# Scores of an attention mixer from 32- and 64-row features in place of stacked 128-row copies

## The chip, the cores and the metric

The kernel runs on one core of a Trainium2 chip. The time is the device time of one execution in microseconds, the lower the better. The engines are PE (matmul), with its weight loads shown apart as PEld, DVE (elementwise work and reductions), ACT (activation functions and copies), POOL (elementwise work) and SP, which issues most of the DMAs.

## The reference

A diffusion backbone of two layers on 256 context tokens and 512 latent tokens, 768 tokens in all, 1024 wide. In each layer one projection feeds three groups of heads that run side by side:

```python
def diff_mixer(...):                 # 4 heads, 2 components of 32 dims each, v of 64
    def attend(q, k, v):
        s = jnp.einsum('bqhcd,bkhcd->bhcqk', q, k) * scale
        p = jax.nn.softmax(s, axis=-1)
        p = p[:, :, 0] - lam * p[:, :, 1]
        return jnp.einsum('bhqk,bkhe->bqhe', p, v)
...
def gqa_attend(q, k, v):             # 6 query heads on 2 key/value heads, 64 dims
    s = jnp.einsum('bqhgd,bkhd->bhgqk', qg, k) * dh ** -0.5
    p = jax.nn.softmax(s, axis=-1)
    o = jnp.einsum('bhgqk,bkhd->bqhgd', p, v)
...
def step(state, xs):                 # gated delta rule: 6 heads of 64 dims, both directions
    v_new = u_i - jnp.einsum('bhck,bhkv->bhcv', w_i, state)
    o_i = jnp.einsum('bhck,bhkv->bhcv', qd_i, state) + jnp.einsum('bhij,bhjv->bhiv', qk_i, v_new)
    state = state * gl_i[..., None, None] + jnp.einsum('bhck,bhcv->bhkv', kd_i, v_new)
```

Latent queries read all 768 keys, context queries the 256 context keys. The last layer needs no context queries. The outputs of the three groups go through one output projection, and a SwiGLU block ends the layer.

## The kernel before

**Numbers in two parts.** Every matmul that must be exact works on split numbers: `hi` is the value rounded to the type fp32r, and `lo` is the value less `hi`. A product is hi·hi + hi·lo + lo·hi. `split` makes the two parts: ACT copies (and so rounds), DVE subtracts.

**The attention stage of a layer.** Its heads are worked in five pairs, in the order `HORD` = 2, 0, 3, 1, 4. Pairs 0 and 1 are two differential heads each; pairs 2, 3 and 4 are two grouped-query heads each, one on either key/value head. The names below are those of the trace's tiles.

- Preparing a differential pair (`attn_prep`): q and k of the pair are loaded (`dq`, `dk`), and `to_feat` transposes them with PE (tile `exp`) and splits them into `qT` and `kT`, hi and lo, with features on the rows: 32 rows for each of 4 components. `stack4` then makes for each component a copy on all 128 rows: PE multiplies the 32 rows by the constant matrix `pick` (tile `stk`; one matmul for the hi, one for the lo part, for 256 and for 512 tokens), and DVE (256 tokens) or ACT (512) copies the result to `qs` or `ks`. The rows of `qs` are [qh, qh, ql, ql], those of `ks` [kh, kl, kh, kl].
- Preparing a grouped-query pair: `stack2` transposes, and copies the 64 rows of each head to both halves of `gqs` (hi in one half, lo in the other) and of two tiles `gks` (hi twice, lo twice), in small operations on 64 rows. The keys are made once in a layer.
- A block (`attend`) is one pair with one tile of 128 queries: a layer-0 pair has six, four with 768 keys and two with 256; a layer-1 pair has four with 768. For each component `scores` fills one of two score buffers (`S`, each of two halves of 384 keys), taken in turn: one matmul for each half on the stacked rows of a differential component, two of a grouped-query head. `softmax` takes the negated maximum on DVE (`nm`) and the exponential with its sum on ACT (`P`). For a differential head DVE then combines the two components (`cR`, and `P<-P,cR`, "the combining step" below). PE transposes `P` three tiles at a time (`pt`), DVE and ACT copy it (`PT`), PE multiplies with the values (`pv`), ACT copies (`OTs`), PE transposes back, and DVE scales into `O`.

**What sets the order.** `mixers` walks through `PLAN`, which mixes the attention's items (`a0` to `a10`) with those of the delta rule: `s0` to `s11` are its twelve steps (tile `scan`, which ends the chain from step to step, and `ops`, its outputs), `p` and `v` prepare it (`mg`, `wps`, `ups`), `o` writes its outputs. `ASTEP` says where in a pair's blocks (`a`) the next pair is prepared: `f` runs the first part of `attn_prep` and `t` the second. A scheduler then orders each engine's instructions by dependences and priorities; the `scan` steps go out at a raised priority. The pools' buffer counts (`ATTN`, here `t` for the stacked copies, `f` for features, `p` for `P`, `q` for `PT`, `g` for `gks`) bound how far ahead the work can run. Each engine executes its queue in order, so that an instruction that waits holds all behind it.

Of the kernel before, what the change touches and what calls it, by code (L numbers as in the profile page):

```python
# [10 lines left out]
F32 = mybir.dt.float32  # L11
# [55 lines left out]
PROJS = (6, 5)  # L67
ATTN = (dict(t=10, f=4, p=4, q=3, v=2, d=2, w=2, g=4, u=1),
        dict(t=10, f=3, p=4, q=4, v=2, d=2, w=2, g=4, u=1))

# [24 lines left out]
class Net:  # L95
# [995 lines left out]

    def to_feat(self, src, t0, name):

        hi, lo = (self.slot(name, F32R, tag="f") for _ in range(2))
# [8 lines left out]
    def pick_setup(self):  # L1103

        self.pick = self.R.tiny("pick", [128, 4, 128], F32R)
        raw = self.slot("pickraw", tag="d")[:, :512]
        self.dma(raw, self.A["pick"])
        self.cp(self.pick.rearrange("p a b -> p (a b)"), raw)

    def parts_of(self, t0):  # L1110

        return ((t0, 2), (2, NT)) if t0 < 2 else ((2, NT),)

    def stack4(self, feat, c, kind, t0, name):

        x = self.slot(name, F32R, tag="t")
        r = slice(32 * c, 32 * c + 32)
        for a, b in self.parts_of(t0):
            ps = self.ring("stk")[:, :128 * (b - a)]
            w = slice(128 * a, 128 * b)  # L1120
            for hl in range(2):
                self.mm(ps, self.pick[r, 2 * kind + hl], feat[hl][r, w], hl == 0, hl == 1)
            if a < 2:
                self.v.tensor_copy(x[:, w], ps)
            else:
                self.cp(x[:, w], ps)
        return x

    def stack2(self, src, t0, name, k):


        out = [[self.slot(name, F32R, tag="g" if k else "t") for _ in range(2 if k else 1)] for _ in range(2)]
        for a, b in self.parts_of(t0):
            ps = self.ring("exp")
            w = slice(128 * a, 128 * b)
            for i in range(a, b):
                self.tr(ps[:, 128 * (i - a):128 * (i - a) + 128], src[:, i])
            for c in range(2):
                own, other = slice(64 * c, 64 * c + 64), slice(64 - 64 * c, 128 - 64 * c)
                p = ps[own, :128 * (b - a)]  # L1140
                hi, lo = out[c][0], out[c][-1]
                self.cp(hi[own, w], p)
                if k:
                    self.cp(hi[other, w], p)
                    self.sub(lo[own, w], p, hi[own, w].bitcast(F32))
                self.sub(lo[other, w], p, hi[own, w].bitcast(F32))
        return out

# [25 lines left out]
    def attend(self, l, pair, O, qts):  # L1174

        for qt in qts:
            nk = TOK if qt >= 2 else CTX
            nkb = nk // 128
            PTs = []
            Z = self.tiny("Z", [128, 2, 2], bufs=4)  # L1180
            for hd, (comps, V) in enumerate(pair):
                Ps = [self.softmax(self.scores(pr, qt, nk), nk, Z[:, hd, ci:ci + 1]) for ci, pr in enumerate(comps)]
                P = Ps[0]
                if len(comps) == 2:
                    c = self.tiny("cR", [128, 1], bufs=4)
                    self.v.reciprocal(out=c, in_=Z[:, hd, 1:2])
                    self.stt(c, c, self.lam[:, l:l + 1], Z[:, hd, 0:1], ALU.mult, ALU.mult)
                    self.stt(P[:, :nk], Ps[1][:, :nk], c, P[:, :nk], ALU.mult, ALU.add)
                PT = self.slot("PT", tag="q")
                for i, k0 in enumerate(range(0, nk, 384)):  # L1190
                    n = min(384, nk - k0)
                    ps = self.ring("pt")
                    for k in range(0, n, 128):
                        self.tr(ps[:, k:k + 128], P[:, k0 + k:k0 + k + 128])
                    if i < EVD[l][len(comps) - 1]:
# [7 lines left out]
            for kb in range(nkb):  # L1203
                for c in range(2):
                    self.mm(pv[64 * c:64 * c + 64, :128], pair[c][1][:, kb], PTs[c][:, 128 * kb:128 * kb + 128], kb == 0, kb == nkb - 1)
            OT = self.R.tiny("OTs", [128, 128], bufs=2)
# [5 lines left out]
    def attn_prep(self, l, i):  # L1212


        t0 = 2 if l == DEPTH - 1 else 0
        if i < 2:
            q = self.load_tok(self.dqk[:, :, 128 * i:128 * i + 128], t0, "dq")
            k = self.load_tok(self.dqk[:, :, 256 + 128 * i:256 + 128 * i + 128], 0, "dk")
            q = self.to_feat(q, t0, "qT")
# [5 lines left out]
            yield [(comps[2 * c:2 * c + 2], vs[:, :, 64 * c:64 * c + 64]) for c in range(2)]  # L1225
            return
        if self.gks is None:
            self.gks = self.stack2(self.load_tok(self.dkv[:, :, 0:128], 0, "gk"), 0, "gks", True)
# [345 lines left out]
def shape_consts():  # L1574
# [26 lines left out]

    pick = np.zeros((4, 32, 4, 4, 32), f)
    for j, at in enumerate(((0, 1), (2, 3), (0, 2), (1, 3))):
        for b in at:
            pick[:, :, j, b] = np.eye(32, dtype=f)
    return {"ident": np.eye(128, dtype=f), "pick": pick.reshape(128, 512), "masks": masks.reshape(128, 768), "mloc": mloc,
            "negm": np.concatenate([negm.reshape(128, 128), masks[:, 2:4].reshape(128, 256)], 1), "blk2": blk2,
# [58 lines left out]
```

## Time and profile before

| | us |
| --- | --- |
| median of the three runs | 2182.35 |
| lowest, highest | 2180.88, 2187.04 |
| the profiled execution | 2187.43 |
| its span, first to last instruction | 2185.6 |

The profile is of one execution. The page's first part gives each engine's busy time and its share of the span. A view by stretches gives, for a stretch of the span, the busy time of each engine with its number of instructions in brackets, then the granted TensorE clock as a share of full speed (1.00 is the upper of its two levels, 2.4 GHz, and 0.50 the lower, 1.2 GHz), the busy share of the DMA engines and what they moved; it can be restricted to the instructions of one tile. The timeline has, for each run of like instructions of one engine, the start in us, the time it took, the engine, the line, the operation, the output and input tiles, the size, the count (xN), and in square brackets the idle time before it and what ended that. The matmuls of one timeline row may not stand next to each other in time where another row's lie between. Over the whole execution the mean granted clock is 0.943.

In this execution layer 0's attention stage lies between about 330 and 620 us, and layer 1's between about 1500 and 1745 us.

### The profile page before, as it was taken

To read this page: it belongs to the slowest core of one execution; us is meant where nothing else is said; L and a number is where in the kernel's file an instruction comes from. 1 tells how busy PE (TensorE), PEld (TensorE's weight loads), DVE (VectorE), ACT (ScalarE), POOL (GpSimd) and SP (SyncE) were. 2 spreads that over 40 slices of the span, in tenths; PEclk is the share of its full clock that TensorE was granted. 3 is DMA by queue.
4 is the path that set the end of the run, shared out by engine and by line. 5 is a ranking of instruction groups with operands and counts; after the bars stand their busy time and mean duration, and the time that the engine had idled before them with its cause. 6 is when DMAs were issued, how large, how long until landed. Compare 5 with 4: busy or idle time off the path is not lost. (4 is left out here: it accounts for less than half of the span.)

```text
span 2185.6 us, 36979 instructions
## 1 busy us (share of the span) xinstructions
PE 2020.9 (92%) x14786; PEld 1672.6 (77%) x14786; DVE 1325.2 (61%) x2223; ACT 823.8 (38%) x1609; POOL 525.0 (24%) x768
## 2 busy tenths in 40 slices
PE   7999877998889999999999989977899799999998
PEld 3788766776668888888888888865676598888887
DVE  6755774575845747565757457687767664443444
ACT  5433315464744321212122344423475653222223
POOL 2403579331014100000000350367323030000002
PEclk9999987698999999999999989987798999999999
DMA  8354434221062324343424411444212242222321
GB/s 296 121 176 132 156 109 113 47 73 35 26 227 78 116 87 154 110 131 102 155 91 140 134 56 48 133 127 125 51 47 60 86 165 77 100 85 92 106 98 61
DMA packets 167596, 236.46 MB, mean 108 GB/s; under 512 B 75328, under 2 KB 109248, under 8 KB 167424
## 3 DMA queue, kind: packets, MB, share of 16 engines
q10 hardware_dynamic: 46160, 144.92, 20.2%
q1 hardware_dynamic: 121264, 89.18, 13.4%
q8 instruction: 116, 1.90, 0.3%
q14 instruction: 56, 0.46, 0.1%
HBM read 198.00 MB, written 36.04 MB: 107 GB/s over the span
## 5 line engine op out<-in xcount | busy, mean ns | idle before, releaser
L185 ACT ACTIVATE whi<-raw 128x1024 fp32r<-128x1024 f32 (+4 forms) x246 | 220.7, 912 | 499.6 <-PE dps L188 207.3
L161 DVE TENSOR_TENSOR wlo<-raw,whi 128x1024 fp32r<-128x1024 f32 (+4 forms) x236 | 250.1, 1074 | 222.1 <-ACT whi L185 221.3
L188 PE MATMUL gu<-ahi,wlo 128*128 128x512 f32 x672 | 264.0, 393 | 1.1 <-DVE wlo L161 1.1
L188 PE MATMUL gu<-ahi,whi 128*128 128x512 f32 x672 | 263.6, 392 | 0.0
L188 PE MATMUL dps<-acth,whi 128*128 128x512 f32 (+1 forms) x560 | 186.6, 348 | 0.4 <-DVE h L179 0.2
L188 PE MATMUL dps<-acth,wlo 128*128 128x512 f32 (+1 forms) x560 | 185.7, 346 | 0.0
L188 PE MATMUL gu<-alo,whi 128*128 128x512 f32 x672 | 168.9, 392 | 0.0
L179 DVE SCALAR_TENSOR_TENSOR junk<-adaw,cb 128x1024 bf16<-128x1024 f32 x112 | 136.8, 1222 | 37.6 <-DMA adaw<-ada_t 36.6
L188 PEld LDWEIGHTS gu<-ahi,wlo 128*128 128x128 f32 x672 | 126.5, 188 | 28.3 <-DVE wlo L161 1.5
L188 PE MATMUL tps<-whi,ahi 128*128 128x512 f32 (+4 forms) x368 | 137.9, 379 | 11.1 <-ACT dq L185 7.2
L188 PEld LDWEIGHTS gu<-alo,whi 128*128 128x128 f32 x672 | 126.3, 188 | 27.6
L179 DVE SCALAR_TENSOR_TENSOR h<-dps,md,h 128x512 f32<-128x512 f32 (+1 forms) x128 | 80.6, 633 | 109.6 <-PE dps L188 109.3
L188 PEld LDWEIGHTS gu<-ahi,whi 128*128 128x128 f32 x672 | 126.5, 188 | 26.7
L188 PE MATMUL tps<-wlo,ahi 128*128 128x512 f32 (+4 forms) x368 | 138.3, 376 | 2.6 <-DVE wlo L161 2.4
L161 POOL TENSOR_TENSOR md<-md,adab 128x2 f32<-128x2 f32 x56 | 32.0, 572 | 439.5 <-DVE junk L179 439.5
L188 PE MATMUL tps<-whi,alo 128*128 128x512 f32 (+4 forms) x368 | 137.3, 373 | 0.0
L1161 DVE TENSOR_REDUCE nm<-S 128x1 f32<-128x768 f32 (+1 forms) x140 | 117.0, 844 | 32.6 <-PE S L188 31.4
L182 ACT ACTIVATE P<-S,nm 128x768 f32<-128x768 f32 (+1 forms) x140 | 114.0, 815 | 51.7 <-DVE nm L1161 46.1
L161 POOL TENSOR_TENSOR sqc<-sqc 128x256 f32<-128x256 f32 x35 | 35.4, 1012 | 397.8 <-ACT sqc L182 397.4
L188 PE MATMUL dps<-actl,whi 128*128 128x512 f32 (+1 forms) x560 | 124.3, 346 | 0.0
L188 PEld LDWEIGHTS dps<-acth,whi 128*128 128x128 f32 x560 | 105.4, 188 | 15.6 <-DVE h L179 0.4
L188 PEld LDWEIGHTS dps<-acth,wlo 128*128 128x128 f32 x560 | 105.7, 189 | 14.3
(295 smaller groups left out, 4629.0 us busy)
## 6 DMA issues: line engine op xcount, KB each, us to landing
raw<-w_u ACTq DMA_DIRECT2D x88, 512.0 KB
adaw<-ada_t ACTq DMA_DIRECT2D x56, 512.0 KB
adaw<-ada_p ACTq DMA_DIRECT2D x24, 512.0 KB
raw<-w_o ACTq DMA_DIRECT2D x24, 512.0 KB
raw<-w_d ACTq DMA_DIRECT2D x44, 256.0 KB
raw<-w_d ACTq DMA_DIRECT2D x32, 320.0 KB
adaq<-ada_q SPq DMA_DIRECT2D x16, 512.0 KB
raw<-w_t ACTq DMA_DIRECT2D x16, 512.0 KB
```

The costliest lines, as they stand in the source:

```text
L161: (eng or self.v).tensor_tensor(out=out, in0=a, in1=b, op=op)
L179: self.v.scalar_tensor_tensor(out=out, in0=a, scalar=sc, in1=b, op0=op0, op1=op1, **k)
L182: self.s.activation(out=out, in_=in_, func=func, **k)
L185: self.s.activation(out=out, in_=in_, func=AF.Copy, **k)
L188: self.t.matmul(out, lhsT, rhs, start=start, stop=stop)
L1161: self.v.tensor_reduce(out=nm, in_=pin, axis=AX.XY if nk == 768 else AX.X, op=ALU.max, negate=True)
```

## The change

The stacked copies go: `pick` with its load, `stack4`, `stack2` and their tiles `qs`, `ks` and `stk`. All q and k, the grouped-query ones too, go through `to_feat` alone. `scores` works on the rows where a component's features lie, 32 rows for a differential component and 64 for a grouped-query head, with three matmuls for each half (hi·hi, hi·lo, lo·hi). It works on two components at once, into the two score buffers: the two of a differential head, or the two heads of a grouped-query block. Their matmuls are issued in turn, one on the rows of the first component and one on the rows of the second. The first score buffer always holds the first component now, where before the two were taken in turn. Buffer counts change in both layers. `O`, `PT` and all behind them are made as before.

```diff
-ATTN = (dict(t=10, f=4, p=4, q=3, v=2, d=2, w=2, g=4, u=1),
-        dict(t=10, f=3, p=4, q=4, v=2, d=2, w=2, g=4, u=1))
+ATTN = (dict(f=8, p=6, q=4, v=2, d=2, w=2, g=2, u=1),) * 2
...
-    def stack4(self, feat, c, kind, t0, name):
-
-        x = self.slot(name, F32R, tag="t")
-        r = slice(32 * c, 32 * c + 32)
-        for a, b in self.parts_of(t0):
-            ps = self.ring("stk")[:, :128 * (b - a)]
-            w = slice(128 * a, 128 * b)
-            for hl in range(2):
-                self.mm(ps, self.pick[r, 2 * kind + hl], feat[hl][r, w], hl == 0, hl == 1)
-            if a < 2:
-                self.v.tensor_copy(x[:, w], ps)
-            else:
-                self.cp(x[:, w], ps)
-        return x
...
-    def scores(self, pairs, qt, nk):
-        ps = self.big("S")
+    def scores(self, feats, rows, qt, nk):
+
+        q, k = feats
+        ps = [self.big("S", j) for j in range(2)]
         halves = 2 if nk == 768 else 1
         w = nk // halves
         for hf in range(halves):
-            for i, (qT, kT) in enumerate(pairs):
-                self.mm(ps[:, hf, :w], qT[:, 128 * qt:128 * qt + 128], kT[:, hf * w:hf * w + w], i == 0, i == len(pairs) - 1)
-        return ps if nk == 768 else ps[:, 0, :nk]
+            for i, (a, b) in enumerate(((0, 0), (0, 1), (1, 0))):
+                for j, r in enumerate(rows):
+                    self.mm(ps[j][:, hf, :w], q[a][r, 128 * qt:128 * qt + 128], k[b][r, hf * w:hf * w + w], i == 0, i == 2)
+        return ps if nk == 768 else [x[:, 0, :nk] for x in ps]
...
-            for hd, (comps, V) in enumerate(pair):
-                Ps = [self.softmax(self.scores(pr, qt, nk), nk, Z[:, hd, ci:ci + 1]) for ci, pr in enumerate(comps)]
+            if not diff:
+                both = self.scores(feats, [r[0] for r in rows], qt, nk)
+            for hd in range(2):
+                ss = self.scores(feats, rows[hd], qt, nk) if diff else [both[hd]]
+                Ps = [self.softmax(x, nk, Z[:, hd, ci:ci + 1]) for ci, x in enumerate(ss)]
...
-            q = [self.stack4(q, c, 0, t0, "qs") for c in range(4)]
-            k = self.to_feat(k, 0, "kT")
-            comps = [[(q[c], self.stack4(k, c, 1, 0, "ks"))] for c in range(4)]
+            k = self.to_feat(self.load_tok(self.dqk[:, :, 256 + 128 * i:256 + 128 * i + 128], 0, "dk"), 0, "kT")
...
+            rows = [[slice(64 * c + 32 * j, 64 * c + 32 * j + 32) for j in range(2)] for c in range(2)]
+            yield (q, k), rows, [vs[:, :, 64 * c:64 * c + 64] for c in range(2)]
...
-        q2 = self.stack2(q, t0, "gqs", False)
-        yield [([[(q2[c][0], k) for k in self.gks[c]]], self.gV[:, :, 64 * c:64 * c + 64]) for c in range(2)]
+        q = self.to_feat(q, t0, "gqs")
+        yield (q, self.gks), [[slice(64 * c, 64 * c + 64)] for c in range(2)], [self.gV[:, :, 64 * c:64 * c + 64] for c in range(2)]
...
-        self.pick_setup()
```

**How the order of the instructions changes.** Below are rows of each engine's queue: line, operation, tiles, size, and the number of like instructions in a row. The code's lines have moved by one between the two kernels (L188 is L187 after it, L191 L190, L889 L888, L915 L914).

On PE in layer 0, before and at the start of the second differential pair; `dk` is that pair's k, `stk` its stacking, and `S<-ks,qs` its scores. In the kernel before:

```order
L191 MATMUL exp<-ident,dk 128x128 x2
L188 MATMUL stk<-qT,pick 128x512 x2
L188 MATMUL stk<-kT,pick 128x256 x2
L191 MATMUL exp<-ident,dk 128x128 x4
L188 MATMUL stk<-kT,pick 128x256 x4
L188 MATMUL stk<-kT,pick 128x512 x2
L188 MATMUL stk<-kT,pick 128x256 x2
L188 MATMUL stk<-kT,pick 128x512 x2
L188 MATMUL S<-ks,qs 128x384 x2
L188 MATMUL stk<-kT,pick 128x512 x2
```

On PE at the same place of the changed kernel, where `pv<-PT,gV` is the end of the grouped-query pair before, and `S<-kT,qT` are the scores of the differential pair:

```order
L187 MATMUL pv<-PT,gV 64x128 x3
L190 MATMUL exp<-ident,dk 128x128 x2
L190 MATMUL pv<-ident,OTs 128x128
L190 MATMUL exp<-ident,dk 128x128 x4
L187 MATMUL S<-kT,qT 128x384 x2
L190 MATMUL otr<-ident,z_6183 128x128 x3
L187 MATMUL S<-kT,qT 128x384 x22
L190 MATMUL pt<-ident,P 128x128 x6
L187 MATMUL S<-kT,qT 128x384 x12
```

The 32 `stk` matmuls that stood between the pair before and its scores are gone, and the first scores stand right behind the six transposes of `dk`; in both kernels the last `scan` of the layer stands ahead of these rows (in the changed one with the rest of the grouped-query pair between).

On DVE, in the same pair, in the kernel before (`nm` is the maximum of one component's scores, `P<-P,cR` the combining step):

```order
L179 SCALAR_TENSOR_TENSOR P<-P,cR 128x768
L1161 TENSOR_REDUCE nm<-S 128x1
L161 TENSOR_TENSOR O<-pv,R 128x128
L1161 TENSOR_REDUCE nm<-S 128x1
L1186 RECIPROCAL cR<-Z 128x1
L179 SCALAR_TENSOR_TENSOR cR<-cR,lam,Z 128x1
L179 SCALAR_TENSOR_TENSOR P<-P,cR 128x768
L1161 TENSOR_REDUCE nm<-S 128x1
```

On DVE at the same place of the changed kernel:

```order
L1148 RECIPROCAL cR<-Z 128x1
L178 SCALAR_TENSOR_TENSOR cR<-cR,lam,Z 128x1
L178 SCALAR_TENSOR_TENSOR P<-P,cR 128x768
L1114 TENSOR_REDUCE nm<-S 128x1 x2
L160 TENSOR_TENSOR O<-pv,R 128x128
L1148 RECIPROCAL cR<-Z 128x1
L178 SCALAR_TENSOR_TENSOR cR<-cR,lam,Z 128x1
L178 SCALAR_TENSOR_TENSOR P<-P,cR 128x768
```

The two maxima of a head stand next to each other now, behind the combining step of the head before; the work on them and their order is otherwise the same.

On PE in layer 1, at the delta rule's last `scan` (`scan<-X,WT`), in the kernel before:

```order
L188 MATMUL stk<-kT,pick 128x512 x2
L188 MATMUL S<-ks,qs 128x384 x2
L915 MATMUL ops<-X,qK 64x64 x8
L889 MATMUL scan<-X,WT 64x64 x12
L188 MATMUL stk<-kT,pick 128x256 x2
L188 MATMUL stk<-kT,pick 128x512 x2
L188 MATMUL S<-ks,qs 128x384 x2
```

On PE at the same place of the changed kernel:

```order
L187 MATMUL pv<-PT,gV 64x128 x6
L914 MATMUL ops<-X,qK 64x64 x11
L187 MATMUL S<-kT,qT 128x384 x6
L190 MATMUL pt<-ident,P 128x128 x3
L888 MATMUL scan<-X,WT 64x64 x12
L190 MATMUL pt<-ident,P 128x128 x3
L187 MATMUL pv<-PT,gV 64x128
L187 MATMUL S<-kT,qT 128x384 x6
```

Of the score matmuls of the second differential pair, 2 of 32 stood ahead of that `scan`, between the stacking matmuls; now 42 of 96 do.

Over both layers, the scores of the kernel before are 144 matmuls for the differential heads (128 of 384 columns, 16 of 256) and 216 for the grouped-query heads (192 and 24); those of the changed one are 432 (384 and 48) and 324 (288 and 36). They stand in 119 runs in PE's queue, of which 75 begin behind a transpose and 47 end before one. Of `stk` 112 matmuls go. The grouped-query keys took 32 small copies and subtractions in both layers together and take 8 on all 128 rows; the queries took 36 in all and take 18.

## Rows read from the trace of the kernel before

**Rows 1.** The page's first part: busy us, share of the span, instructions.

```profile
PE 2020.9 (92%) x14786; PEld 1672.6 (77%) x14786; DVE 1325.2 (61%) x2223; ACT 823.8 (38%) x1609; POOL 525.0 (24%) x768
```

**Rows 2.** By stretches: length; PE, PEld, DVE, ACT, POOL busy; clock; DMA share; GB/s.

```profile
529.50:556.90 27.40, 23.71 (x70) 14.24 (x70) 14.73 (x26) 13.88 (x28) 0.00 (x0) 0.50 0.00 1
556.90:611.50 54.60, 46.96 (x371) 34.35 (x371) 43.92 (x97) 40.12 (x107) 2.27 (x1) 1.00 0.17 56
```

**Rows 3.** By stretches, tile `stk` alone: length; PE, PEld, DVE, ACT busy; clock.

```profile
399.20:422.80 23.60, 12.21 (x32) 6.01 (x32) 3.35 (x8) 4.18 (x7) 0.59 0.21 48
526.00:545.50 19.50, 12.25 (x32) 6.62 (x32) 3.40 (x8) 4.76 (x8) 0.59 0.00 0
1549.00:1571.00 22.00, 8.79 (x20) 3.98 (x20) 1.69 (x4) 3.81 (x7) 0.50 0.20 44
1653.70:1676.40 22.70, 8.39 (x24) 4.31 (x24) 1.65 (x4) 4.10 (x8) 0.70 0.15 37
```

**Rows 4.** Timeline of PE: two places with stacking matmuls, layer 0.

```profile
403.29 1.21 PE L188 MATMUL stk<-qT,pick 32*128 32x512 f32 x4 [0.69 <-ACT qs L185]
...
538.74 1.22 PE L188 MATMUL stk<-kT,pick 32*128 32x512 f32 x2 [0.40 <-ACT ks L185]
```

**Rows 5.** Timeline, layer 0, from the last `scan` to the second differential pair.

```profile
506.82 0.52 PE L889 MATMUL scan<-X,WT 64*64 64x64 f32 x12
...
526.06 0.50 PE L188 MATMUL stk<-qT,pick 32*128 32x256 f32 x2
...
533.90 1.11 PE L191 MATMUL exp<-ident,dk 128*128 128x128 f32 x4 [0.25 <-ACT qs L185]
...
540.94 0.96 DVE L1161 TENSOR_REDUCE nm<-S 128x1 f32<-128x768 f32 x1 [2.13 <-PE S L188]
```

**Rows 6.** Timeline of PE in the second differential pair, layer 0.

```profile
558.07 0.55 PE L191 MATMUL pt<-ident,P 128*128 128x128 f32 x3
558.37 0.60 PE L188 MATMUL S<-ks,qs 128*128 128x384 f32 x2
558.81 0.27 PE L191 MATMUL pv<-ident,OTs 128*128 128x128 f32 x1
...
560.53 0.52 PE L191 MATMUL pt<-ident,P 128*128 128x128 f32 x3
560.98 0.33 PE L188 MATMUL pv<-PT,vs 128*64 128x128 f32 x2
```

**Rows 7.** Timeline of DVE and ACT in the same pair.

```profile
549.51 0.96 DVE L1161 TENSOR_REDUCE nm<-S 128x1 f32<-128x768 f32 x1 [0.90 <-PE S L188]
...
560.47 0.89 ACT L182 ACTIVATE P<-S,nm 128x768 f32<-128x768 f32 x1
...
562.05 1.02 DVE L179 SCALAR_TENSOR_TENSOR P<-P,cR 128x768 f32<-128x768 f32 x1
562.99 0.95 DVE L1161 TENSOR_REDUCE nm<-S 128x1 f32<-128x768 f32 x1
```

**Rows 8.** Timeline of PE and DVE, last grouped-query pair of layer 0.

```profile
585.17 0.94 PE L188 MATMUL S<-gks,gqs 128*128 128x384 f32 x4
585.95 0.27 PE L191 MATMUL pv<-ident,OTs 128*128 128x128 f32 x1
586.15 0.96 DVE L1161 TENSOR_REDUCE nm<-S 128x1 f32<-128x768 f32 x1
...
598.55 1.99 DVE L1161 TENSOR_REDUCE nm<-S 128x1 f32<-128x768 f32 x2
```

**Rows 9.** Timeline of PE, layer 1: last `scan`, last scores of the second differential pair.

```profile
1669.08 1.55 PE L889 MATMUL scan<-X,WT 64*64 64x64 f32 x24
...
1707.02 0.92 PE L188 MATMUL S<-ks,qs 128*128 128x384 f32 x2 [0.64 <-ACT P L182]
```

**Rows 10.** Timeline of PE at the start of layer 0's attention.

```profile
333.71 1.54 PE L191 MATMUL exp<-ident,gk 128*128 128x128 f32 x6 [9.15 <-DMA gk<-dkv]
...
345.76 2.93 PE L188 MATMUL S<-gks,gqs 128*128 128x384 f32 x8
```

More of the change, by code (lines that the diff above doesn't have):

```diff
@@ L1090, in lam_prep, with to_feat @@
         self.ts(self.lam[:, l:l + 1], self.lam[:, l:l + 1], 1.0, -lam_init(l), ALU.mult, ALU.add, eng=self.g)
-    def to_feat(self, src, t0, name):
-        hi, lo = (self.slot(name, F32R, tag="f") for _ in range(2))
+    def to_feat(self, src, t0, name, tag="f"):
+        hi, lo = (self.slot(name, F32R, tag=tag) for _ in range(2))
         for a, b in ((t0, 2), (2, NT)) if t0 < 2 else ((2, NT),):
@@ L1101, in to_feat @@
         return hi, lo
[L1103 to L1112, printed above, removed]
-    def stack4(self, feat, c, kind, t0, name):
-        x = self.slot(name, F32R, tag="t")
-        r = slice(32 * c, 32 * c + 32)
-        for a, b in self.parts_of(t0):
-            ps = self.ring("stk")[:, :128 * (b - a)]
-            w = slice(128 * a, 128 * b)
-            for hl in range(2):
-                self.mm(ps, self.pick[r, 2 * kind + hl], feat[hl][r, w], hl == 0, hl == 1)
-            if a < 2:
-                self.v.tensor_copy(x[:, w], ps)
-            else:
-                self.cp(x[:, w], ps)
-        return x
[L1129 to L1147, printed above, removed]
     def load_tok(self, src, t0, name, tag="d"):
@@ L1169, in scores @@
         for hf in range(halves):
-            for i, (qT, kT) in enumerate(pairs):
-                self.mm(ps[:, hf, :w], qT[:, 128 * qt:128 * qt + 128], kT[:, hf * w:hf * w + w], i == 0, i == len(pairs) - 1)
-        return ps if nk == 768 else ps[:, 0, :nk]
+            for i, (a, b) in enumerate(((0, 0), (0, 1), (1, 0))):
+                for j, r in enumerate(rows):
+                    self.mm(ps[j][:, hf, :w], q[a][r, 128 * qt:128 * qt + 128], k[b][r, hf * w:hf * w + w], i == 0, i == 2)
+        return ps if nk == 768 else [x[:, 0, :nk] for x in ps]
     def attend(self, l, pair, O, qts):
+        feats, rows, vs = pair
+        diff = len(rows[0]) == 2
         for qt in qts:
@@ L1180, in attend @@
             Z = self.tiny("Z", [128, 2, 2], bufs=4)
-            for hd, (comps, V) in enumerate(pair):
-                Ps = [self.softmax(self.scores(pr, qt, nk), nk, Z[:, hd, ci:ci + 1]) for ci, pr in enumerate(comps)]
+            if not diff:
[3 more added lines that the diff above has]
+                Ps = [self.softmax(x, nk, Z[:, hd, ci:ci + 1]) for ci, x in enumerate(ss)]
                 P = Ps[0]
-                if len(comps) == 2:
+                if diff:
                     c = self.tiny("cR", [128, 1], bufs=4)
@@ L1194, in attend @@
                         self.tr(ps[:, k:k + 128], P[:, k0 + k:k0 + k + 128])
-                    if i < EVD[l][len(comps) - 1]:
+                    if i < EVD[l][diff]:
                         self.v.tensor_copy(PT[:, k0:k0 + n], ps[:, :n])
@@ L1204, in attend @@
                 for c in range(2):
-                    self.mm(pv[64 * c:64 * c + 64, :128], pair[c][1][:, kb], PTs[c][:, 128 * kb:128 * kb + 128], kb == 0, kb == nkb - 1)
+                    self.mm(pv[64 * c:64 * c + 64, :128], vs[c][:, kb], PTs[c][:, 128 * kb:128 * kb + 128], kb == 0, kb == nkb - 1)
             OT = self.R.tiny("OTs", [128, 128], bufs=2)
@@ L1216, in attn_prep @@
         if i < 2:
-            q = self.load_tok(self.dqk[:, :, 128 * i:128 * i + 128], t0, "dq")
-            k = self.load_tok(self.dqk[:, :, 256 + 128 * i:256 + 128 * i + 128], 0, "dk")
-            q = self.to_feat(q, t0, "qT")
+            q = self.to_feat(self.load_tok(self.dqk[:, :, 128 * i:128 * i + 128], t0, "dq"), t0, "qT")
             yield
-            q = [self.stack4(q, c, 0, t0, "qs") for c in range(4)]
-            k = self.to_feat(k, 0, "kT")
-            comps = [[(q[c], self.stack4(k, c, 1, 0, "ks"))] for c in range(4)]
+            k = self.to_feat(self.load_tok(self.dqk[:, :, 256 + 128 * i:256 + 128 * i + 128], 0, "dk"), 0, "kT")
             vs = self.load_tok(self.dkv[:, :, 256 + 128 * i:256 + 128 * i + 128], 0, "vs", "v")
-            yield [(comps[2 * c:2 * c + 2], vs[:, :, 64 * c:64 * c + 64]) for c in range(2)]
+            rows = [[slice(64 * c + 32 * j, 64 * c + 32 * j + 32) for j in range(2)] for c in range(2)]
+            yield (q, k), rows, [vs[:, :, 64 * c:64 * c + 64] for c in range(2)]
             return
         if self.gks is None:
-            self.gks = self.stack2(self.load_tok(self.dkv[:, :, 0:128], 0, "gk"), 0, "gks", True)
+            self.gks = self.to_feat(self.load_tok(self.dkv[:, :, 0:128], 0, "gk"), 0, "gks", "g")
             self.gV = self.load_tok(self.dkv[:, :, 128:256], 0, "gV", "u")
@@ L1600, in rope @@
         return np.ascontiguousarray(t.transpose(1, 0, 2, 3))
[L1602 to L1606, printed above, removed]
+    return {"ident": np.eye(128, dtype=f), "masks": masks.reshape(128, 768), "mloc": mloc,
             "negm": np.concatenate([negm.reshape(128, 128), masks[:, 2:4].reshape(128, 256)], 1), "blk2": blk2,
```

## The prediction

> **What bounds the kernel now.** I read the page first: TensorE (PE) is busy 92% of the span [rows 1], so an edit is worth what it does to PE's queue, or to a wait in it. Outside the two attention stages (about 330 to 620 us and 1500 to 1745 us, one for each layer) the change touches nothing, so I read only these. Each has two parts. In the first, attention is mixed with the delta-rule steps (tiles `mg`, `wps`, `ups`, `scan`). After the last `scan` attention stands alone, and everything behind waits for its last tile. In layer 0 the last `scan` is at 506.82 us [rows 5]; in layer 1 it is at 1669.08 [rows 9]. In the stretch where attention stands alone no engine is full: from 556.9 to 611.5 PE is busy 46.96 of 54.6 us, DVE 43.92, ACT 40.12 [rows 2]. What ends there is a chain: scores on PE, maximum on DVE, exponential on ACT, transposes on PE.
>
> **What is removed.** The stacking matmuls `stk` and the copies behind them run four times. In their four stretches PE is busy with `stk` for 12.21, 12.25, 8.79 and 8.39 us, together 41.6, and the granted clock is between 0.50 and 0.70 of full speed there, so for much of it the lower of the two levels, 1.2 GHz [rows 3]. ACT and DVE spend 16.8 and 10.1 us on the copies, partly beside PE. Three of the four stretches lie in the mixed parts; the second stands alone.
>
> **Layer 0, after the last scan.** The last `scan` starts at 506.82, the old pair's last transposes and products reach 526, then `stk` starts at 526.06, and the first maximum of the second differential pair is at 540.94 [rows 5]: 34 us with hardly a softmax. In the changed order on PE only the rest of the pair before, six transposes `exp` and their split stand between that `scan` and the scores. The six transposes take about 1.8 us (the four of 1.11 us at the lower clock in [rows 5] are two thirds of them); the two rounds of rounding and subtracting behind them I put at 2 us, and the last round of transposing, copying and multiplying of the pair before at 4 us, both plain estimates. So about 8 us stand where 34 stood, and scores can begin about 25 us earlier, if the `scan` itself comes when it did. The bounds are 12 (only the `stk` part, from 526.06 to 540.94 less 3) and 28.
>
> **What is added: more scores.** The kernel has 32 differential heads with 768 keys, each with two components (16 in each layer), and 24 grouped-query blocks with 768 keys and two heads (12 in each layer). A differential head now takes 4 matmuls of 384 columns and will take 12, on two groups of 32 rows. A grouped-query block takes 8 and will take 12, on two groups of 64. What this costs hangs on whether the two groups run at the same time. The trace has an accidental case: at 538.74 two `stk` matmuls of 512 columns on one row group take 1.22 us at the lower clock; at 403.29, at the same clock, four take 1.21 us, two of 512 on one row group and two of 256 on another, with their output in different banks [rows 4]. The second pair is free. So I count pairs: 6 in place of 4 matmuls and 6 in place of 8. Two matmuls hold PE 0.44 us (558.37 to 558.81, [rows 6]) and four 0.78 (585.17 to 585.95, [rows 8]), so one more is 0.17. That gives 32 x 2 x 0.17 = +10.9 and 24 x 2 x 0.17 = -8.2; the blocks of 256 keys (8 heads with one more, 6 blocks with one less) cancel to within 1 us. Net +3.
>
> **What is added: changes of shape.** Scores of 128 rows stand among transposes of 128 rows now; scores on 32 or 64 rows are another shape. Three transposes `pt` followed by scores take 0.30 us until the scores start (558.07 to 558.37), followed by the products `pv`, which have 64 columns, 0.45 (560.53 to 560.98) [rows 6]: a change costs 0.15 us. In the changed order 75 of 119 runs of scores follow a transpose and 47 are followed by one: 122 x 0.15 = +18. The Trainium skill, "TensorEngine Tiling (Array Packing)", Key Properties, says that a change of tiling mode, not of the tile alone, drains TensorE, and it speaks against this change. The trace agrees in that the 0.15 us is there; a reader who takes the drain as free would have these 18 us less. PE's sum is then -42 + 3 + 18 = -21 us over both stages, of which only a part lies on the path.
>
> **What is added: two components at a time.** The scores of both components now go into the two score buffers together, so the next two can start only when both exponentials have been taken; before, each buffer was refilled by itself. Behind the waiting matmul stands all of PE's queue, and the scheduler has put other rows there in some places only. The chain of a differential head becomes: from the end of the second exponential to the next maximum 1.63 us (560.47 + 0.89 to 562.99: the small reads and the combining step of 1.02 on DVE; the six pairs of scores run beside it), the first maximum 0.95, the first exponential with its read 1.10, the second 0.90, and 0.1 for handing over: 4.7 us [rows 7]. The changed order on DVE does put the combining step ahead of the next maximum. Now eight maxima follow one another from 549.51 to 562.99, seven steps of 1.93, so 3.85 us a head. That is +0.85 a head where attention stands alone, 8 heads in layer 0: +7. A grouped-query block becomes 1.6 + 0.95 + 1.1 + 0.9 = 4.6; now six steps from 586.15 to 598.55 make 4.1 a block [rows 8]: +0.5, four blocks, +2; heads of 256 keys +1. Layer 0 alone: -25 + 10 = **-15**.
>
> **Layer 1, after the last scan.** At 1669.08 only 2 of 32 score matmuls of the second differential pair have run, and the last two start at 1707.02 [rows 9]: 38 us for 3.75 blocks, with `stk` in between. In the changed order 42 of 96 stand ahead of the last `scan`, so 2.25 blocks are left: 4.5 heads x 4.7 = 21 us. That is -17, and +2 for the grouped-query blocks: **-15**.
>
> **Starts.** The first scores of layer 0 come 12 us after the first transpose of k (333.71 to 345.76, [rows 10]), behind 24 small copies and subtractions (8 and 8 for k, 4 and 4 for q, on 64 partitions each) that become 8, and behind the load of `pick`. The delta-rule work fills some of this. I take -3 of a possible -14 for both layers.
>
> **Mixed parts.** They lose 29 us of `stk` on PE (three stretches), gain about two thirds of the 21 us of scores and changes of shape (14), and take in the work that the two ends lose (about 2.5 blocks of some 5.6 us on PE, 14): net near zero on PE. But the two-at-a-time chain is there too, and a waiting score holds up `scan`. I take **+8**, between -15 and +30, nearer to PE's sum because other PE work fills these parts.
>
> **The sum.** -15 - 15 - 3 + 8 = -25 us. Against the profiled execution (2187.4 us, span 2185.6) that is 2162; that execution lies 5 us above the median of 2182.35, so for the median 2157.
>
> **Rivals.** (a) *The clock comes back as well.* The four `stk` stretches are also where the granted clock is low: 0.50 from 529.5 to 556.9 and 1.00 right after [rows 2]. If the lower level goes with `stk`, other PE work there (some 40 us, an estimate) doubles in speed, and the mixed parts shrink: another -25, 2132. Against it: small tiles of the delta rule stand in the same stretches, and scores on 32 rows replace scores on 128. (b) *The waiting second component decides.* Each score pair holds PE from the end of the first exponential to the end of the second, 1.1 us, wherever its first matmuls stand next to each other. In the mixed parts there are some 40 pairs: +44 in place of the +8, 2193; it overturns the gain once more than about 30 of the 40 are held. The same hold would slow the `scan` chain, for 2200 as its middle. For it: scores already wait for ACT's exponential now, 0.64 us at 1707.02 [rows 9]. Against it: the changed order splits many runs with other rows in between. (c) *The row groups run one after the other.* Then 378 pairs cost 0.17 more, +64: 2221. Against it stands [rows 4]. (d) *The change does not do what it says for time*: the ends' gain goes into a later last `scan`, and the result is within 6 us of 2182.
>
> **How the numbers follow.** Forecast 2157 with 0.52; (a) 2132 with 0.16; (b) 2200 with 0.15; (c) 2221 with 0.04; (d) 0.13. A difference of 0.3%, 6.5 us, is about what a measurement of this kernel can tell from none. Faster 0.68, within 0.13, slower 0.19. The range takes in most of (a), all of (d) and the lower half of (b): 2128 to 2196.
>
> **What would show it.** In the changed profile: no `stk`; scores that start in pairs less than 0.02 us apart and six pairs in about 1.2 us; scores of the second differential pair within 10 us of layer 0's last `scan`; maxima in twos, 4.7 us a head; and the last `scan` no later than 507 and 1665. A last `scan` some 20 us later, PE waiting for the exponential in the mixed parts, or a granted clock at the lower level through the differential blocks would make the prediction wrong.

## The result and the profile after

The changed kernel takes 2256.51 us in the median (2236.69 to 2263.77), the kernel before 2184.69, over four executions of each. The ratio is 1.0315, with a 95% interval of 1.0243 to 1.0387: slower by 72 us, where 25 us faster was forecast (2157 against the 2182.35 of the three runs known then). The profiled execution of the changed kernel is its fastest, 2236.69 us with a span of 2234.9. What is read from it below is therefore the smaller part of the loss.

The page's first part, which answers to [rows 1], and the group of the maxima (`S` the scores, `nm` their maximum):

```profile
PE 2082.2 (93%) x15070; PEld 1733.7 (78%) x15070; DVE 1309.0 (59%) x2178; ACT 799.5 (36%) x1554; POOL 528.9 (24%) x768
...
L1114 DVE TENSOR_REDUCE nm<-S 128x1 f32<-128x768 f32 (+1 forms) x140 | 115.5, 845 | 94.4 <-PE S L187 94.1
```

In the kernel before:

```profile
L1161 DVE TENSOR_REDUCE nm<-S 128x1 f32<-128x768 f32 (+1 forms) x140 | 117.0, 844 | 32.6 <-PE S L188 31.4
```

PE is busy 61 us longer than before, where the prediction's sum had 21 us less. DVE waits 94 us for scores ahead of its maxima (31 us before). DVE and ACT are busy 16 and 24 us less than before, POOL 4 us more.

Where the time lies shows by stretches: the mixed part of layer 0, what stands alone behind its last `scan`, and the same two of layer 1. The columns are those of [rows 2]. The kernel before:

```profile
330.00:507.10 177.10, 159.51 (x2368) 124.98 (x2370) 110.79 (x218) 101.68 (x244) 92.33 (x139) 0.83 0.30 74
507.10:608.00 100.90, 87.39 (x586) 60.05 (x581) 67.39 (x147) 61.60 (x156) 6.86 (x5) 0.86 0.12 40
1512.00:1670.30 158.30, 139.27 (x2194) 108.01 (x2196) 110.80 (x221) 84.50 (x194) 56.62 (x72) 0.84 0.24 57
1670.30:1725.00 54.70, 50.87 (x377) 38.05 (x374) 43.52 (x84) 38.18 (x88) 4.58 (x4) 0.88 0.08 25
```

The changed kernel, with the second differential pair of layer 0 as a line of its own at the end:

```profile
330.00:552.10 222.10, 202.56 (x2536) 159.66 (x2536) 108.50 (x209) 95.59 (x236) 90.01 (x133) 0.73 0.21 53
552.10:654.00 101.90, 94.08 (x547) 71.02 (x544) 57.97 (x122) 49.98 (x124) 6.84 (x5) 0.72 0.09 30
1553.00:1728.00 175.00, 154.44 (x2351) 123.84 (x2350) 114.58 (x229) 84.42 (x194) 56.29 (x73) 0.83 0.23 56
1728.00:1773.00 45.00, 45.00 (x346) 33.95 (x341) 32.58 (x64) 30.56 (x71) 4.58 (x4) 1.00 0.10 30
...
561.30:619.30 58.00, 55.66 (x231) 43.42 (x231) 29.51 (x55) 24.39 (x57) 0.00 (x0) 0.50 0.03 11
```

The mixed parts grow by 45 and 17 us. Behind the last `scan` layer 0 gains nothing (+1) and layer 1 gains 10. The column to read is the clock. In layer 0 it falls from 0.83 to 0.73 and from 0.86 to 0.72. In the second differential pair of layer 0 PE is busy 55.66 of 58 us and has the lower level, 1.2 GHz, all the time. The kernel before ran the first blocks of that pair at the lower level too, and those from 556.9 us on at the upper one ([rows 2]). In layer 1 the clock does not fall in this execution: 0.84 and 0.83 in the mixed part, 0.88 and 1.00 behind it.

The timeline of PE in the changed kernel shows the second thing, which the code does not let one expect:

```profile
330.81 2.11 PE L187 MATMUL S<-gks,gqs 64*128 64x384 f32 x12
...
565.88 3.16 PE L187 MATMUL S<-kT,qT 32*128 32x384 f32 x12 [2.07 <-ACT P L181]
568.98 1.54 PE L190 MATMUL pt<-ident,P 128*128 128x128 f32 x6
570.45 3.34 PE L187 MATMUL S<-kT,qT 32*128 32x384 f32 x12
...
633.90 1.33 PE L187 MATMUL S<-gks,gqs 64*128 64x384 f32 x6
635.16 1.20 PE L190 MATMUL pt<-ident,P 128*128 128x128 f32 x9
636.29 1.31 PE L187 MATMUL S<-gks,gqs 64*128 64x384 f32 x6
```

At 330.81 twelve matmuls take 2.11 us at the lower clock: two at a time. At 570.45 twelve take 3.34 us at the same clock, so a good part of them run one by one. At 633.90 six of one head, a transposing run, and six of the other head follow one another, 0.176 us each at the upper clock. The scheduler has taken the turns apart: the first component's buffer comes free earlier, so its matmuls are put into the queue as soon as they may run. Of 756 score matmuls 124 start within 0.04 us of the one before them, where 378 would if all stood in turn.

### The profile page after: what moved, and what is told of

It is laid out like the page before. It is cut to its first block, busy times and chain, and to the rows that moved or that the text cites. A ratio compares the mean times of both kernels' runs of the same rounds, so it can differ in the third digit from the quotient of the medians.

```text
span 2234.9 us, 37446 instructions
## 1 busy us (share of the span) xinstructions
PE 2082.2 (93%) x15070; PEld 1733.7 (78%) x15070; DVE 1309.0 (59%) x2178; ACT 799.5 (36%) x1554; POOL 528.9 (24%) x768
## 5 line engine op out<-in xcount | busy, mean ns | idle before, releaser
L187 PE MATMUL gu<-ahi,wlo 128*128 128x512 f32 x672 | 263.8, 393 | 1.2 <-DVE wlo L160 1.2
L187 PE MATMUL gu<-ahi,whi 128*128 128x512 f32 x672 | 263.6, 392 | 0.0
L187 PE MATMUL dps<-acth,whi 128*128 128x512 f32 (+1 forms) x560 | 186.5, 347 | 0.4 <-DVE h L178 0.2
L187 PE MATMUL dps<-acth,wlo 128*128 128x512 f32 (+1 forms) x560 | 185.5, 346 | 0.0
L187 PE MATMUL gu<-alo,whi 128*128 128x512 f32 x672 | 168.8, 392 | 0.0
L187 PEld LDWEIGHTS gu<-ahi,wlo 128*128 128x128 f32 x672 | 126.5, 188 | 28.3 <-DVE wlo L160 1.5
L187 PEld LDWEIGHTS gu<-alo,whi 128*128 128x128 f32 x672 | 126.2, 188 | 27.6
L187 PE MATMUL tps<-whi,ahi 128*128 128x512 f32 (+4 forms) x368 | 137.1, 377 | 11.2 <-ACT dq L184 7.2
L187 PEld LDWEIGHTS gu<-ahi,whi 128*128 128x128 f32 x672 | 126.5, 188 | 26.8
L187 PE MATMUL tps<-wlo,ahi 128*128 128x512 f32 (+4 forms) x368 | 137.8, 375 | 1.9 <-DVE wlo L160 1.7
L187 PE MATMUL tps<-whi,alo 128*128 128x512 f32 (+4 forms) x368 | 136.4, 371 | 0.0
L187 PE MATMUL dps<-actl,whi 128*128 128x512 f32 (+1 forms) x560 | 124.2, 346 | 0.0
L190 PE MATMUL pt<-ident,P 128*128 128x128 f32 x520 | 106.8, 333 | 15.3 <-ACT P L181 8.2
L187 PEld LDWEIGHTS dps<-acth,whi 128*128 128x128 f32 x560 | 105.3, 188 | 15.6 <-DVE h L178 0.4
```

Source lines behind the costliest of these rows:

```text
L187: self.t.matmul(out, lhsT, rhs, start=start, stop=stop)
L190: self.t.transpose(out, in_, self.ident)
```

## Experiments

All times are medians. Ratios are to the kernel before in the same comparison. "Span x clock" multiplies the profiled span by the mean granted clock: a rough yardstick for what the execution would take with the clock always at the upper level. It is rough because only PE's time scales with the clock. The last three columns are those of the profiled execution, which need not be the median one: the changed kernel's is its fastest, e5_diff's its slowest.

| kernel | us | ratio (95%) | span, clock | span x clock | PE busy |
| --- | --- | --- | --- | --- | --- |
| before | 2184.69 | 1 | 2185.6, 0.943 | 2061 | 2020.9 |
| changed | 2256.51 | 1.0315 (1.0243 to 1.0387) | 2234.9, 0.926 | 2070 | 2082.2 |
| e1_turn | 2234.86 | 1.0213 (1.0172 to 1.0253) | 2227.0, 0.927 | 2064 | 2030.5 |
| e3_nostk | 2136.63 | 0.9759 (0.9728 to 0.9790) | 2136.8, 0.949 | 2028 | 1973.4 |
| e4_more128 | 2248.48 | 1.0281 (1.0250 to 1.0311) | 2239.0, 0.949 | 2125 | 2077.7 |
| e5_diff | 2216.96 | 1.0138 (1.0082 to 1.0195) | 2232.4, 0.919 | 2052 | 2080.6 |
| e6_gqa | 2238.50 | 1.0236 (1.0219 to 1.0253) | 2239.2, 0.927 | 2076 | 2074.4 |
| e7_rows128 | 2155.87 | 0.9862 (0.9839 to 0.9885) | 2149.6, 0.966 | 2077 | 2012.4 |
| e8_rows64 | 2273.88 | 1.0372 (1.0334 to 1.0411) | 2276.6, 0.903 | 2056 | 2110.6 |
| e9_twos | 2167.54 | 0.9915 (0.9898 to 0.9932) | 2163.5, 0.952 | 2060 | 1966.4 |
| e10_dma | 2159.44 | 0.9873 (0.9853 to 0.9893) | 2159.9, 0.948 | 2048 | 1978.2 |
| e11_zeros | 2185.04 | 0.9988 (0.9974 to 1.0002) | 2176.5, 0.965 | 2100 | 2015.1 |
| e12_dmapool | 2175.24 | 0.9938 (0.9917 to 0.9959) | 2175.4, 0.945 | 2056 | 1975.1 |
| e13_early | 2154.49 | 0.9847 (0.9830 to 0.9864) | 2147.0, 0.954 | 2048 | 1970.3 |

**e1_turn: the turns kept in PE's queue.** An order edge from each score matmul of the changed kernel to the one before it, the later buffer's first.

```diff
-                for j, r in enumerate(rows):
...
+                for j in (1, 0):
...
+                    if tail is not None:
+                        self.tc.add_manual_dep(x.ins, tail.ins.name, mybir.DependencyInfo(mybir.DependencyClass.NoSync, mybir.DependencyReason.DATA), reason="turn")
+                    tail = x
```

> The changed kernel, with the score matmuls of both row groups chained in PE's queue, so that one of each group stands next to the other everywhere (33 runs of 12 where the changed kernel has 47 runs of 6). Theory 'in series' (the scheduler has put three or six matmuls of one row group in a row, since the first buffer comes free first; two groups that do not alternate run one after the other): the pairs overlap, PE's busy time falls from 2082 by some 45 us, and the time comes to 2190 to 2215. Theory 'clock' (matmuls on 32 and 64 rows let the granted clock fall): the clock stays between 0.91 and 0.93, and the time above 2235. Theory 'held in twos' (a score waits for both buffers and holds PE's queue): the chain makes the hold stricter, 2260 or more.

```profile
583.48 2.29 PE L1129 MATMUL S<-kT,qT 32*128 32x384 f32 x12
```

This row answers to 570.45 above: twelve such matmuls at the same clock take 2.29 us in place of 3.34. 367 of the 378 pairs start within 0.04 us of each other now, 124 in the changed kernel. PE's busy time falls by 52 us, as expected, but the time only by some 22, to 2235, and the intervals of the two kernels just touch. The mean clock stays where it was (0.927), as the theory "clock" said. Matmuls in series are real, and they are not the main part.

**e3_nostk, e4_more128: the two sides of the sum on full rows.**

```diff
 e3_nostk
     def stack4(self, feat, c, kind, t0, name):
...
+        return feat[c % 2]
 e4_more128
+            pairs = (pairs * 3)[:3]
             for i, (qT, kT) in enumerate(pairs):
```

> The kernel before, with the stacking left out: the features themselves stand in for the stacked copies, so the differential scores are other numbers; four more feature buffers, four fewer for copies. If the prediction's step on the removal is right, this alone is worth 25 to 45 us: 2140 to 2160. If the removal only uncovers another chain, it is under 10 us: 2175 or more.

> The kernel before, with each differential score matmul issued three times and each grouped-query one one and a half times, all on 128 rows: as many score matmuls as in the changed kernel, in series, with the stacking still there; the scores are other numbers. Theory 'in series': the count is the price, 396 more x 0.176 us = 70 us on PE, of which some 45 to 65 show: 2230 to 2250, at a granted clock near 0.94. Theory 'clock': the count on full rows costs little, 2185 to 2215, and the clock does not fall.

The removal alone is worth 49 us, a little more than expected. The count of score matmuls alone, in series on 128 rows, costs 63 us, at a clock that does not fall (0.949).

**e5_diff, e6_gqa: one half of the change each.** The other half keeps its stacked copies and its `scores` of before; the buffer counts are each run's own.

> Only the differential half of the change: rows of 32 and two components at once, while the grouped-query pairs keep their stacked copies and their two matmuls a half. Theory 'in series': 288 of the 396 added matmuls are here, and the gain of the removed stacking too: 2215 to 2240, so most of the loss. Theory 'clock': the differential blocks on 32 rows stay at the lower clock as in the changed kernel (0.51 from 570 to 620 us), 2240 or more. If the grouped-query half is what costs: 2190 or less.

> Only the grouped-query half of the change: rows of 64, two heads at once, while the differential pairs keep their stacked copies. Theory 'in series': 108 more matmuls, 19 us, less the small copies saved: 2185 to 2205. Theory 'clock and shape': 64 rows let the clock fall as 32 do, 2205 to 2230. If the two halves simply add up to the whole (72, of which the differential half gave 31), 2225.

The differential half costs 31 us, though the 49 of the removal lie in it; the grouped-query half costs 53, more than any branch said. Together they are 85, the whole is 72. In e6 the clock is 0.927. The time at the lower level, worked out as twice (1 - clock) x span, rises from 249 to 327 us. Half of these 78 us is 39, and 108 more matmuls at 0.176 are 19: together 58 against the 53 measured.

**e7_rows128: the changed kernel on full rows.** This is the experiment that decides.

```diff
-                    self.mm(ps[j][:, hf, :w], q[a][r, 128 * qt:128 * qt + 128], k[b][r, hf * w:hf * w + w], i == 0, i == 2)
+                    self.mm(ps[j][:, hf, :w], q[a][:, 128 * qt:128 * qt + 128], k[b][:, hf * w:hf * w + w], i == 0, i == 2)
```

> The changed kernel, every score matmul on all 128 rows of its operands (the scores are sums over all the components, so other numbers): the same buffers, the same two components at a time, as many matmuls, but no pair can overlap and no change of shape stands against the transposes. Theory 'clock and shape' (what is left of the loss beside the matmuls in series comes from the lower clock and the changes of shape): the clock rises to about 0.945 and the time comes to 2190 to 2215, which is the 2137 without stacking and the 63 of the extra matmuls. Theory 'held in twos': shape does not matter, 2245 to 2280, with the clock at 0.92 or less.

The same number of matmuls, the same buffers, no pair that can overlap, and no change of shape between scores and transposes: 2156 us, 100 us less than the changed kernel. By stretches:

```profile
330.00:503.90 173.90, 159.34 (x2509) 131.46 (x2506) 103.21 (x204) 93.50 (x233) 89.11 (x134) 0.95 0.26 66
503.90:594.00 90.10, 79.97 (x598) 64.79 (x595) 60.49 (x127) 51.06 (x127) 7.35 (x6) 0.92 0.11 34
1500.00:1657.70 157.70, 150.13 (x2396) 127.24 (x2396) 121.01 (x242) 89.00 (x205) 55.97 (x67) 0.96 0.24 60
1657.70:1689.50 31.80, 31.80 (x271) 27.27 (x268) 24.11 (x48) 24.16 (x55) 4.58 (x4) 1.00 0.15 43
```

The clock is 0.95, 0.92, 0.96 and 1.00: above that of the kernel before in each stretch, and above the changed kernel's in all but the last, where that had 1.00 as well. The time at the lower level is 146 us, against 331 in the changed kernel. Half of the difference is 92 us; the two spans differ by 85. By span x clock e7 has slightly more to do (2077 against 2070). The expected 2190 to 2215 was the theory's direction with too small a clock: at 0.945 these 2077 would be 2197.

**e8_rows64: the kernel before on 64 rows.** The reverse: nothing changed but the rows of the score matmuls.

```diff
-                self.mm(ps[:, hf, :w], qT[:, 128 * qt:128 * qt + 128], kT[:, hf * w:hf * w + w], i == 0, i == len(pairs) - 1)
+                self.mm(ps[:, hf, :w], qT[:64, 128 * qt:128 * qt + 128], kT[:64, hf * w:hf * w + w], i == 0, i == len(pairs) - 1)
```

> The kernel before, with every score matmul on the first 64 of its 128 rows (so other numbers): as many matmuls, one after the other as before, the stacking still there, each component's buffer by itself. Nothing is in series that was not before. It prices the shape alone: the drains at each change of shape and the clock. Theory 'clock and shape': the time at the lower clock rises from 252 us by 40 to 90, and the run comes to 2215 to 2250; if only the drains count, PE's work at the upper clock rises by some 15 to 25 us, the lower-clock time stays near 250, and the run comes to 2195 to 2210. If shape is free: 2185.

```profile
330.00:543.50 213.50, 191.67 (x2368) 144.16 (x2368) 110.83 (x217) 101.22 (x242) 92.16 (x137) 0.71 0.24 60
543.50:653.00 109.50, 96.52 (x587) 64.15 (x582) 68.03 (x148) 63.35 (x158) 6.84 (x5) 0.81 0.12 37
1562.00:1750.30 188.30, 170.72 (x2192) 131.38 (x2192) 110.84 (x220) 86.42 (x194) 51.57 (x65) 0.67 0.20 49
1750.30:1817.00 66.70, 63.46 (x385) 43.21 (x382) 46.31 (x88) 39.63 (x89) 5.19 (x5) 0.77 0.07 21
```

With the same count of matmuls in each stretch, PE is busy 32 and 31 us longer in the mixed parts, the clock there is 0.71 and 0.67 in place of 0.83 and 0.84, and the kernel takes 87 us more. That is above all that was expected. Span x clock is 2056 against 2061: at an equal clock nothing would be left, so the drains at the changes of shape, which are there too, do not show in the sum.

**e9_twos: the hold alone.** e3_nostk with both components' scores in one chained run.

> The kernel before without stacking (features stand in for the copies, so other numbers), with both components' scores put into the two buffers in one chained run on PE, the second buffer's first. All matmuls on 128 rows, as many as before. It prices the hold alone, against 2137 without the chain. Theory 'held in twos': 2165 to 2230. Otherwise the hold is small: 2125 to 2150.

31 us over e3_nostk, at the lower edge of what "held in twos" said. PE's time outside its busy time rises by about as much, from 163 (2136.8 less 1973.4) to 197 us. So e1_turn's chain gave 52 us of PE's time and took most of it back: there PE's idle time rose from 153 to 197. What two components at a time cost without the chain no run here shows by itself.

**e10_dma, e12_dmapool, e13_early, e11_zeros: can the gain of the removal be had?** e10 keeps the stacked copies and full rows, and has DMAs make them from the features; e12 issues them from POOL's queue; e13 is e10 with k's step one block earlier. e11 is the changed kernel with q laid out with zeros by POOL, so that its scores run on all 128 rows (`blk` is 1 on a component's rows and 0 elsewhere).

```diff
 e10_dma, in stack4
-            ps = self.ring("stk")[:, :128 * (b - a)]
...
+        for g in range(4):
+            self.dma(x[32 * g:32 * g + 32, 128 * t0:TOK].bitcast(F32), feat[g % 2 if kind else g // 2][r, 128 * t0:TOK].bitcast(F32))
 e13_early
-ASTEP = ("aaoayfaaat", "afaoytaa")
+ASTEP = ("aaoayfaata", "afatoyaa")
 e11_zeros, in scores
+        m = self.blk[:, c0:c0 + 2].unsqueeze(2).to_broadcast([128, 2, 128])
...
+            self.mul(qz[a], q[a][:, 128 * qt:128 * qt + 128].bitcast(F32).unsqueeze(1).to_broadcast([128, 2, 128]), m, self.g)
```

> The kernel before, with the stacked copies made by DMA, four DMAs of 32 rows for each component, in place of PE, ACT and DVE; the same numbers are computed. If the stacking's price is PE's time and its place in PE's queue, and the transfers are in time, it comes near the 2137 of the kernel without stacking: 2135 to 2160. If the transfers end late or hold up the delta rule's loads on the same queue: 2185 or more.

> The kernel before with the stacked copies made by DMA, issued from POOL's queue in place of SP's. If SP's queue (where the delta rule's loads stand behind the copies) holds back the 22 us between 2159 and the 2137 without stacking: 2135 to 2155. If POOL's own work is held up by waiting for the features: 2165 or more.

> The kernel with the stacked copies made by DMA (2159), with each pair's second preparation step (k and its copies) one block earlier, in both layers. In the trace of the DMA kernel PE waits 15.2 us, 9 times, for the copies of k. If these waits are what lies between 2159 and the 2137 without stacking, most of them go: 2140 to 2153. If the earlier copies meet the delta rule's loads, or the features are no earlier, it stays within 2155 to 2170.

> The changed kernel with its scores on all 128 rows: for each block POOL lays out q with zeros on the rows of the other components, so that the same numbers are computed; all else of the change stays, with one buffer fewer for P and for PT. Theory 'clock and shape': as fast as the changed kernel on full rows (2156), so 2150 to 2175, with a granted clock of 0.955 or more. If POOL's products come late: 2180 to 2220 at that clock.

e10 is 26 us faster than the kernel before with the same numbers computed, e13 34 us. The waits of the score matmuls in e10 and, behind it, in e13:

```profile
  DMA ks<-kT: 15.2, 9
```

```profile
  DMA ks<-kT: 4.6, 3
```

Most of the wait goes, but the intervals of the two (0.9853 to 0.9893, 0.9830 to 0.9864) overlap, so the step from one to the other is not shown. Issued from POOL the copies cost about 15 us against e10. Whether POOL's own work or the copies come late there stays open. e11 gets the clock that was expected (0.965) and is 71 us faster than the changed kernel, but lands on the kernel before, not on e7's 2156. It has 140 products on POOL of about 0.61 us each, for which its score matmuls wait 3.7 us in all, and fewer buffers; which of the two costs the 29 us stays open.

## Why the prediction was wrong

**The term that failed is one that was not in the sum: the clock.** The prediction saw the lower level at the `stk` matmuls on 32 rows, and wrote as rival (a) that it might go with them. Against this it noted that scores on 32 rows replace scores on 128, and priced that at no gain, instead of asking what the same rows would do to the clock in all the blocks. e7 and e8 turn nothing but the rows, and what hangs on them, in both directions: -100 and +87 us. The four executions of the changed kernel differ in the same way. Spans of 2234.9, 2249.9, 2259.4 and 2262.0 us go with clocks of 0.926, 0.921, 0.912 and 0.911, and with span x clock between 2061 and 2072. Two of the signs in the prediction's list of what would refute it came about: the lower level through the differential blocks, in layer 0, and a later last `scan`, by 45 us there. In layer 1 of the profiled execution the blocks of the second differential pair kept the upper level (last section), so fewer rows lowered the clock on the whole and not in every stretch.

**"So I count pairs"** failed as well. Two groups of rows do run at once where they stand next to each other, as [rows 4] had it (330.81 above). But the changed order shows runs of six where turns would give twelve (its rows of layer 1), and the prediction counted the runs without asking which matmuls stood in them; the twelve at 570.45 stand in one run and are not in turn either. Rival (c) was right for a large part of them: 254 of 378 do not start together. Keeping the turns is worth some 22 us of time and 52 of PE's.

**What was removed** held, and was undersized: 49 us alone (e3).

**Changes of shape, +18.** The row was read rightly: in the changed kernel a score starts 0.20 us after the start of the transpose before it at the upper clock, in e7 0.03. The Trainium skill's drain ("TensorEngine Tiling (Array Packing)", Key Properties) agrees with that. But in e8, where each run of scores pays it, span x clock did not rise. The term is below what the runs can tell.

**Two components at a time, +10.** The mechanism as written is not there: each buffer is freed by itself, and the first component's six matmuls do not wait for the second exponential. The scores at 565.88 (above) start while it is still running:

```profile
565.73 0.89 ACT L181 ACTIVATE P<-S,nm 128x768 f32<-128x768 f32 x1
```

The combining steps of the changed kernel, in the second pair of layer 0, the first three and the last of the eight with 768 keys:

```profile
567.20 1.02 DVE L178 SCALAR_TENSOR_TENSOR P<-P,cR 128x768 f32<-128x768 f32 x1
...
571.94 1.02 DVE L178 SCALAR_TENSOR_TENSOR P<-P,cR 128x768 f32<-128x768 f32 x1
...
576.60 1.02 DVE L178 SCALAR_TENSOR_TENSOR P<-P,cR 128x768 f32<-128x768 f32 x1
...
612.13 1.02 DVE L178 SCALAR_TENSOR_TENSOR P<-P,cR 128x768 f32<-128x768 f32 x1
```

In e7, the first four and the last:

```profile
528.25 1.01 DVE L178 SCALAR_TENSOR_TENSOR P<-P,cR 128x768 f32<-128x768 f32 x1
...
532.99 1.02 DVE L178 SCALAR_TENSOR_TENSOR P<-P,cR 128x768 f32<-128x768 f32 x1
...
536.39 1.02 DVE L178 SCALAR_TENSOR_TENSOR P<-P,cR 128x768 f32<-128x768 f32 x1
...
539.79 1.02 DVE L178 SCALAR_TENSOR_TENSOR P<-P,cR 128x768 f32<-128x768 f32 x1
...
556.53 1.02 DVE L178 SCALAR_TENSOR_TENSOR P<-P,cR 128x768 f32<-128x768 f32 x1
```

In the kernel before, the first and the last:

```profile
545.50 1.02 DVE L179 SCALAR_TENSOR_TENSOR P<-P,cR 128x768 f32<-128x768 f32 x1
...
573.48 1.01 DVE L179 SCALAR_TENSOR_TENSOR P<-P,cR 128x768 f32<-128x768 f32 x1
```

The first two steps are 4.7 us, the head that the prediction had, and this is met by accident: PE is the bound there, at the lower clock (12 scores and 6 transposes, 3.34 and 1.54 us, above). Over the eight heads the mean is 6.4 us. In e7 a head takes 3.4 us where nothing else lies between, and 4.0 in the mean, as in the kernel before (4.0), which had the lower clock for the first of them. So on full rows a head does not come to the 4.7 us, and on few rows it comes to more through PE: the clock and the matmuls in series.

**The two ends.** Scores of the second pair start 8.6 us behind layer 0's last `scan` (560.75 less 552.1; about 8 forecast), yet the stretch behind it is no shorter, since the clock falls in it: +1 for -15. Layer 1 has -10 for -15. On full rows (e7), at a higher clock than before, they are -11 and -23, so the reading of the queue is not what failed.

**The mixed parts, +8 between -15 and +30,** measured +62. In layer 0 the clock falls (0.83 to 0.73). In layer 1 of this execution it does not, and PE is busy 15 us longer, which is most of the 17; matmuls in series are the likely cause. In e7 the two are -3 and -1.

That e7 comes to 2156, where 2157 was forecast, confirms no sum: e7 has no pairs that overlap, and a higher clock than the forecast had.

## What to carry to other kernels

Before splitting a matmul of 128 rows into smaller row groups, look in the trace at the granted clock where the kernel already runs on few rows, and price the whole stage at that clock; a busy PE did not always keep its clock here. Turns that a scheduler may reorder are not turns: look at each run in the new order and name the matmuls in it, and weigh an order edge against what it holds up. A copy that feeds full-row matmuls may be worth keeping; give it to the engine that is idle, here the DMAs.

## What the runs showed of the hardware

In layer 0's second differential pair of the changed kernel the lower clock level stood through 58 us in which PE was busy 55.66, with scores on 32 rows among transposes. In e7, with the scores on 128 rows, the clock was down as well when that pair began, and came back in its blocks:

```profile
510.00:530.00 20.00, 15.18 (x59) 10.97 (x60) 9.80 (x21) 5.38 (x12) 3.25 (x3) 0.66 0.07 20
530.00:594.00 64.00, 59.38 (x468) 49.55 (x467) 45.37 (x97) 43.10 (x109) 2.27 (x1) 1.00 0.10 34
```

The rows alone do not settle it. All score matmuls of layer 1's second differential pair are on 32 rows as well. In the changed kernel they ran from 1710.6 to 1753.4 us at the upper level; in e5_diff, where this half of the change is the same, those from 1712 us on ran at the lower one. First the changed kernel, then e5_diff:

```profile
1710.60:1753.40 42.80, 42.39 (x441) 33.31 (x439) 37.89 (x76) 26.99 (x62) 10.67 (x10) 1.00 0.16 45
```

```profile
1712.00:1760.00 48.00, 47.42 (x232) 36.28 (x231) 22.35 (x41) 20.13 (x45) 4.62 (x4) 0.50 0.09 28
```

PE is busy nearly all the time in both. So fewer rows lowered the mean clock and the speed of whole executions (e7, e8), but what decides the level of a single stretch stays open.

The Trainium skill, "TensorE: Matmul & The Clock Gate", Part 1, gives the lower level as the idle state and the upper as the busy one. The two rows at the lower level (55.66 of 58 us, 47.42 of 48) do not agree with it, if busy is read as the time that PE is occupied; the row of layer 1 at the upper level does. Whether row groups that overlap do better than one alone stays open too: in e1_turn nearly all overlap, and its clock was 0.927.
